# Two low columns ride behind the high columns: the z product's first token set at 260, 256 and 258 columns

## The chip, the cores and the metric

The kernel runs on one core of a Trainium2 chip. The metric is the device time of one launch in microseconds (us), as a median over runs. Inside a run, a profiler records every instruction of the core's engines: the tensor engine (PE, with its weight loads listed apart as PEld), the vector engine (DVE), the scalar engine (ACT), GpSimd (POOL) and the engine that issues most transfers (SP).

## The reference

One layer of a hybrid decoder: 16 meta tokens are put ahead of 1024 tokens, the 1040 rows are normalised, and one wide product `z` feeds two branches (windowed attention and a gated convolution), which are merged by gates. A convolutional feed-forward network follows.

```python
h = layer_norm(concatenate([meta, x], axis=1), in_ln_g, in_ln_b)
z = h @ w_in + b_in
q, k, v, c_in, gates = split(z)          # 512, 128, 128, 1024, 2048 columns
y_attn = swa_sink_attention(q, k, v, ...) @ w_attn_proj
c_val, c_gate = split(c_in)
y_conv = silu(layer_norm(causal_dwconv(c_val * sigmoid(c_gate)))) @ w_conv_proj
g_attn, g_conv = split(gates)
mixed = sigmoid(g_attn) * y_attn + sigmoid(g_conv) * y_conv
h = layer_norm(ALPHA * h + mixed @ w_out)
up = causal_dwconv(h @ ffn_w_up); u, g = split(up)
out = layer_norm(ALPHA * h + (gelu(g) * u) @ ffn_w_down)[:, 16:]
```

The meta rows are dropped from the output. Behind `z`, only the last two meta tokens (rows 14 and 15) are still needed for gates and queries, since the feed-forward convolution has 3 taps.

## The kernel before, in words

Products are computed in a reduced float32 type on PE, and each operand is split into a high part and a low part: high times high, high times low, low times high, three matmuls for each chunk of 128 contracted channels (function `product`, L303 to L316: L310 is high weights on high tokens, L314 high weights on low tokens, L315 low weights on high tokens). The contraction of 1024 channels has 8 chunks, so a set of tokens takes 24 matmuls, all summed in one PSUM tile.

The 30 tiles of 128 columns of `w_in` are the weights (`whi`, `wlo`), the normalised tokens, transposed, are the moving operand. They lie in two SBUF tiles, RHO for chunks 0 to 3 and RHC for chunks 4 to 7; `h0(k, hl, a, b)` (L267) gives the columns a to b of chunk k, high (hl 0) or low (hl 1). The columns of the first 272 tokens lie in a region of their own, one block of 272 words for each pair of chunk and part; the other 768 tokens lie in blocks of 768 words ahead of it. In the built program both tiles begin 64 bytes past a multiple of 128 bytes. So the second token set begins on such a multiple (word 16 + 768 i), and the first set's needed columns, from token 14, begin 72 or 8 bytes past one.

Tokens are taken in three sets, `ZG` = 0 to 272, 272 to 528, 528 to 1040. For queries 1 to 3 and the 16 gate tiles the first set begins at token 14 (`TG`), which makes it 258 columns; for the convolution's tiles it has 272. `z_group` (L318) takes a PSUM tile `ps_z`, of which there are 3 in turn, and hands it to an evacuation: a gate's is one ACT instruction with tanh and a store (L714, L715), a query's one ACT instruction (L362) and then a split into high (ACT, `qsh`) and low (DVE, `qsl`).

At the start of the program the order of work on PE, ACT and DVE is written out by hand (`in_order`). There, `parts(g, k)` (L510 to L517) splits the transposed tokens of a set into high and low parts, one cast and one subtraction for each chunk; the first set's parts (`FA` to RHO and RHC, 272 columns) are written into the row of the last set's (`tm`, 384 columns), while PE runs the first product of the last set (L550). After that a scheduler orders the work by ranks: the evacuations come first, the splits of weights (L279 on ACT, L282 on DVE) next, then attention, then the tiles of z, and the convolution's taps on DVE (L707, 120 instructions on 1026 columns) last. Attention's matmuls are set among the tiles of z.

Of the kernel before, what the change touches and what calls it, by code (L numbers as in the profile page):

```python
# [25 lines left out]
AF = mybir.ActivationFunctionType  # L26
OP = mybir.AluOpType
# [4 lines left out]
KC = D // P  # L32
NMETA = 16
S = 1024
T = S + NMETA
U0 = 14
U = T - U0
HD = 64
# [63 lines left out]
def tile_hybrid_layer(  # L102
# [3 lines left out]
    nc = tc.nc  # L106
# [5 lines left out]
    def load(o, i):  # L112
        return nc.sync.dma_start(out=o, in_=i)

    def store(o, i):

        return nc.scalar.dma_start(out=o, in_=i)

    def f32(ap):
        return ap.bitcast(F)  # L120

    def after(ins, first):

        tc.add_manual_dep(ins.ins, first.ins.name, mybir.DependencyInfo(
            mybir.DependencyClass.NoSync, mybir.DependencyReason.SCHED_ONLY), reason="order of work")

    @contextmanager
    def rank(p):

        saved = tc.cur_priority  # L130
        tc.cur_priority = p
        yield
        tc.cur_priority = saved
# [34 lines left out]
    start = ExitStack()  # L168
# [39 lines left out]
    def bcol(m):  # L208
        return colA[:, m:m + 1]
# [13 lines left out]
    qb = const.tile([P, 4], F, name="qb")  # L223
# [42 lines left out]

    def h0(k, hl, a, b):  # L267
        i = (k % 4) * 2 + hl
        o = 6196 + i * 272 if a < 272 else 16 + i * 768 - 272
        return (RHO if k < 4 else RHC)[:, o + a:o + b]  # L270


# [14 lines left out]
    def weights(shape, fill):  # L287
        fills[0] += 1
        n = fills[0]
        own = n == 3  # L290
        raw = sp.tile(shape, F, name="wr3") if own else wraw(shape)
        with rank({1: 13, 2: 18, 3: 17, 4: 23}.get(n, RK_SPLIT)):
            last_fill.append(fill(raw))
        hi, lo = (sp.tile(shape, R, name=t + "3") if own else wsp_p.tile(shape, R, name=t, tag=t)
                  for t in ("whi", "wlo"))
        if n <= 3:
            return hi, lo, raw
        with rank(RK_SPLIT):
            last_split.append(split(raw, hi, lo, True))
        return hi, lo  # L300
# [2 lines left out]

    def product(ps, terms, behind=None, lead=None):

        n = len(terms)
        if lead is not None:
            nc.tensor.matmul(ps[:, :64], terms[0][0], lead, start=True, stop=True)
        for i, (ah, al, bh, bl) in enumerate(terms):
            ins = nc.tensor.matmul(ps, ah, bh, start=i == 0, stop=False)  # L310
            chunks_done.append(ins)
            if i == 0 and behind is not None:
                after(ins, behind)
            nc.tensor.matmul(ps, ah, bl, start=False, stop=False)  # L314
            last = nc.tensor.matmul(ps, al, bh, start=False, stop=i == n - 1)  # L315
        return last  # L316

    def z_group(wt, g, a, b, evac):  # L318
        hi, lo = wt
        ps = pat.tile([P, 512], F, name="ps_z", tag="mm", bufs=3)  # L320
        product(ps[:, :b - a], [(hi[:, k], lo[:, k], h0(k, 0, a, b), h0(k, 1, a, b)) for k in range(KC)])
        with rank(RK_EVAC):
            evac(g, a, b, ps[:, :b - a])

    def z_tile(fill, groups, evac, wt=None):
        wt = wt or weights([P, KC, P], fill)
        for g, (a, b) in enumerate(groups):
            z_group(wt, g, a, b, evac)

    def in_cols(m):  # L330
        return lambda raw: load(raw, w_z[m])
# [5 lines left out]
    def stage(n):  # L337
        o = st_next[0] if st_next[0] + n <= 2040 else 0
        st_next[0] = o + n
        return FA[:, 4104 + o:4104 + o + n]  # L340
# [17 lines left out]

    def q_evac(r):
        def evac(g, a, b, ps):  # L360
            t = stage(b - a)
            nc.scalar.activation(t, ps, AF.Identity, bias=qb[:, r:r + 1], scale=HD ** -0.5)  # L362
            cut = b - a if g == 0 else 256
            for x in range(0, b - a, cut):
                parts_of(r, g, t[:, x:min(b - a, x + cut)], a + x)
        return evac

    def parts_of(r, g, t, a):
        n = t.shape[-1]
        h, l = (qsp.tile([P, 272], R, name=x, tag=x)[:, :n] for x in ("qsh", "qsl"))  # L370
        nc.scalar.copy(h, t)
        nc.vector.tensor_tensor(l, t, f32(h), OP.subtract)
        for hl, (put, x) in enumerate(((store, f32(h)), (load, f32(l)))):
            c = 0
            if g == 0:
                c = 2
                load(dram(qd, (hl * 4 + r) * 2, [[8 * U, P], [1, 2]]), x[:, :2])
            m = (n - c) // P
            i = (a - U0 + c) // P
            put(dram(qd, q_at(i) + (hl * 4 + r) * HD, [[8 * U, P], [4 * P, 2 * m], [1, HD]]),  # L380
                x[:, c:].rearrange("p (n q) -> p n q", q=HD))
# [13 lines left out]
    V = nc.vector  # L395
# [113 lines left out]
    def parts(g, *ks, hi_act=()):  # L509
        a, b = HG[g]  # L510
        for k in ks:
            tm = tms[g, k]
            if k in hi_act:
                ac(nc.scalar.copy(h0(k, 0, a, b), tm))
            else:
                dv(V.tensor_copy(h0(k, 0, a, b), tm))
            dv(V.tensor_tensor(h0(k, 1, a, b), tm, f32(h0(k, 0, a, b)), OP.subtract))  # L517

    first = [weights([P, KC, P], in_cols(m)) for m in (4, 5, 0)]
    evacs0 = [k_evac, v_evac, q_evac(0)]  # L520
# [11 lines left out]
    def span(i, g):  # L532
        a, b = HG[g]
        return (U0 if i == 2 and g == 0 else a), b
# [30 lines left out]
    def evac(g, *tiles):  # L565
        for i in tiles:
            a, b = span(i, g)
            with rank(RK_EVAC):
                evacs0[i](g, a, b, sums0[i])
# [50 lines left out]
    for k in range(8):  # L620
        scaled(1, k)
        parts(1, k, hi_act=(k,))
        if k == 1:
            whi0(1)
            wlo0(1)
        if k in (3, 6):
            stat(4, 6 if k == 3 else 7)
# [10 lines left out]
    for k in range(8):  # L638
        scaled(2, k)
        parts(2, k, hi_act=(1, 3, 5, 7))  # L640
        if k in (3, 4, 5, 6):
            parts(0, 2 * k - 6, 2 * k - 5)
# [5 lines left out]
    for a, b in ((0, 400), (400, J_LEN)):  # L648
        ps = pat.tile([P, 512], F, name="ps_v", tag="o" if a == 0 else "t", bufs=1 if a == 0 else 2)
# [20 lines left out]
    V = ap.tile([P, NB, NKV, 2, HD], R, name="v")  # L670
# [3 lines left out]
    bias = ap.tile([P, 2, NH // 2, KW], F, name="bias")  # L674
# [34 lines left out]
    def gate_tile(i):  # L709
        b2, m = divmod(i, KC)  # L710

        def gate_evac(g, a, b, ps):
            t = stage(b - a)
            nc.scalar.activation(t, ps, AF.Tanh, bias=bcol(14 + i), scale=0.5)  # L714
            store(sgd[b2, m, :, a - U0:b - U0], t)  # L715

        z_tile(in_cols(14 + i), TG, gate_evac)
# [28 lines left out]
    ps = pat.tile([P, 512], F, name="ps_vm", tag="t", bufs=2)  # L746
# [4 lines left out]
    for q4 in range(2):  # L751
        ps = pat.tile([P, 512], F, name="ps_v4", tag="t", bufs=2)
# [4 lines left out]
        for g in range(NKV):  # L757
            hi, lo = (V[:, q4 * 4:q4 * 4 + 4, g, i] for i in range(2))
# [35 lines left out]
    ps = pat.tile([P, 512], F, name="ps_s2", tag="t", bufs=2)  # L794
    for h in range(NH):
        g, r = divmod(h, 4)
        o = ps[:2, h * 16:(h + 1) * 16]
# [34 lines left out]
    for g in range(NKV):  # L832
        ps = pat.tile([P, 512], F, name="ps_t2", tag="t", bufs=2)
# [3 lines left out]
        hi, lo = (t[:16, g * 8:g * 8 + 8].rearrange("p (r q) -> p r q", r=4) for t in p2)  # L837
        nc.scalar.copy(hi, src)
        nc.vector.tensor_tensor(lo, src, f32(hi), OP.subtract)
    for g in range(NKV):  # L840
        o = po[:, g * 8:g * 8 + 8]
# [21 lines left out]
    for i in range(NB):  # L863
        for g in range(NKV):
# [299 lines left out]
    for m in range(KC):  # L1164
        hi, lo = weights([P, KC, P], lambda raw: load(raw, w_ab[m]))
# [403 lines left out]
    for c in range(FC):  # L1569
# [8 lines left out]
        for subs in passes:  # L1578
            last = subs == passes[-1]
            w_next = iter(range(7))  # L1580
            a, b = SUB[subs[0]][0], SUB[subs[-1]][1]
            i = max(a, 2)

            def at(t, a=a):
                return t[:, 254 + a:254 + b]
# [34 lines left out]
            ins = tt(c11[:, a:b], at(Z), u13[:, a:b], OP.add)  # L1620
# [23 lines left out]
            ins = tt(c22[:, i:b], c22[:, i:b], u13[:, i:b], OP.add)  # L1644
# [286 lines left out]
```

## Time and profile before

| | |
|---|---|
| median of 3 runs | 1236.19 us (1235.96 to 1236.53) |
| profiled execution, first to last instruction | 1234.6 us (its time around that is not listed; median less span is 1.6 us) |
| granted PE clock | 0.999 |
| PE busy | 1225.2 us, 99% |
| DVE busy | 1085.2 us, 88% |
| ACT busy | 584.7 us, 47% |
| PE in the stretch 55 to 405 us (tiles of z and attention) | 350.0 of 350.0 us |
| DVE in that stretch | 324.2 of 350.0 us |
| ACT in that stretch | 156.6 of 350.0 us |

[...] The distance from one start to the next is what a matmul costs in a dense row, and it is read from the list of instructions in order of time. In that list, equal instructions that follow each other share a row, and a figure in brackets is the idle time ahead of a row with what ended it. Some matmul records are missing from a trace.

### The profile page before, as it was taken

How to read it: one execution, taken by the hardware profiler on the slowest of the kernel's cores; microseconds unless marked ns; L12 is line 12 of the kernel's file. 1: busy time of each engine (PE TensorE's matmuls, PEld its weight loads, DVE VectorE, ACT ScalarE, POOL GpSimd, SP SyncE). 2: the span in 40 equal slices, each digit the busy share in tenths (PEclk: the TensorE clock that was granted, in tenths of full speed). 3: DMA queues.
4: the chain of work that ended last, by engine and by line, in shares of the span. 5: the costliest groups of instructions: out<-in, count | busy, mean ns of one | idle time of the engine just before them, and what ended most of it. 6: DMA issues, size and time to landing. Idle time of an engine off the chain costs nothing.

```text
span 1234.6 us, 21810 instructions
## 1 busy us (share of the span) xinstructions
PE 1225.2 (99%) x8568; PEld 1141.5 (92%) x8568; DVE 1085.2 (88%) x1842; ACT 584.7 (47%) x1065; POOL 15.6 (1%) x20
## 2 busy tenths in 40 slices
PE   9999999999999999999999999999999999999997
PEld 8999989999999999888999999999999998888886
DVE  8899989999879798659899999998999986996697
ACT  7532336654255223345755545555455554445331
POOL 1000000000000010000000000000000000000000
PEclk9999999999999999999999999999999999999999
DMA  7396834412255655322255555554455568988722
GB/s 282 74 298 151 210 98 116 127 55 73 82 158 163 183 140 144 104 85 87 66 171 207 191 187 205 188 183 142 172 203 190 178 239 304 391 315 312 256 86 85
DMA packets 109152, 213.02 MB, mean 173 GB/s; under 512 B 31883, under 2 KB 46779, under 8 KB 108922
## 3 DMA queue, kind: packets, MB, share of 16 engines
q1 hardware_dynamic: 93050, 200.56, 49.5%
q10 hardware_dynamic: 16000, 11.07, 2.9%
q8 instruction: 67, 1.10, 0.4%
q14 instruction: 35, 0.29, 0.1%
HBM read 149.98 MB, written 62.70 MB: 172 GB/s over the span
## 4 chain that ended last, share of the span: by engine, by line
PE 98%; DVE 1%; ACT 0%; issue 0%; DMA 0%; POOL 0%; DVEq 0%; POOLq 0%
PE px L1599 14%; PE py L1599 9%; PE ps_x L1745 9%; PE ps_z L315 8%; PE ps_z L314 8%; PE ps_z L310 8%; PE ps_z L1745 8%; PE pw L1599 5%; PE pz L1599 5%; PE ps_p L310 2%; PE ps_p L314 2%; PE ps_p L315 2%; PE ps_w L310 2%; PE ps_w L315 2%; PE ps_w L314 2%; PE ps_z L550 2%
## 5 line engine op out<-in xcount | busy, mean ns | idle before, releaser
L707 DVE SCALAR_TENSOR_TENSOR FA<-cin,cols,FA 128x1026 f32<-128x1026 f32 x120 | 152.2, 1277 | 0.9
L315 PE MATMUL ps_z<-RHO,wlo 128*128 128x256 f32 (+2 forms) x324 | 103.5, 320 | 0.0
L314 PE MATMUL ps_z<-RHO,whi 128*128 128x256 f32 (+2 forms) x324 | 103.4, 319 | 0.0
L315 PE MATMUL ps_z<-RHC,wlo 128*128 128x256 f32 (+2 forms) x324 | 103.4, 319 | 0.0
L314 PE MATMUL ps_z<-RHC,whi 128*128 128x256 f32 (+2 forms) x324 | 103.4, 319 | 0.0
L310 PE MATMUL ps_z<-RHO,whi 128*128 128x256 f32 (+2 forms) x324 | 103.3, 319 | 0.0
L310 PE MATMUL ps_z<-RHC,whi 128*128 128x256 f32 (+2 forms) x324 | 103.2, 319 | 0.0
L279 ACT CAST whi<-wr 128x1024 fp32r<-128x1024 f32 x37 | 38.9, 1050 | 107.4 <-PE ps_z L314 85.5
L1408 ACT CAST RHO<-wr 128x512 fp32r<-128x512 f32 x92 | 55.3, 619 | 25.3 <-DVE wr L1426 11.7
L1409 DVE TENSOR_TENSOR RHO<-wr,RHO 128x512 fp32r<-128x512 f32 x92 | 61.8, 684 | 5.1 <-ACT RHO L1408 5.0
L310 PEld LDWEIGHTS ps_z<-RHO,whi 128*128 128x128 f32 x324 | 60.9, 188 | 4.3
L314 PEld LDWEIGHTS ps_z<-RHO,whi 128*128 128x128 f32 x324 | 61.0, 188 | 4.2
L310 PEld LDWEIGHTS ps_z<-RHC,whi 128*128 128x128 f32 x324 | 60.9, 188 | 4.1
L314 PEld LDWEIGHTS ps_z<-RHC,whi 128*128 128x128 f32 x324 | 61.0, 188 | 4.0
L315 PEld LDWEIGHTS ps_z<-RHO,wlo 128*128 128x128 f32 x324 | 60.9, 188 | 4.0
L315 PEld LDWEIGHTS ps_z<-RHC,wlo 128*128 128x128 f32 x324 | 61.0, 188 | 3.9
L1426 DVE TENSOR_TENSOR wr<-wr 128x512 f32<-128x512 f32 x88 | 59.9, 681 | 0.2
L282 DVE TENSOR_TENSOR wlo<-wr,whi 128x1024 fp32r<-128x1024 f32 x35 | 42.7, 1220 | 11.8 <-ACT whi L279 11.4
L1611 ACT COPY FA<-px 128x514 f32<-128x514 f32 (+2 forms) x23 | 13.2, 572 | 70.7 <-PE px L1599 70.6
L1408 ACT CAST ws<-wr 128x512 fp32r<-128x512 f32 x60 | 36.1, 618 | 18.8 <-DVE wr L1426 10.7
L714 ACT ACTIVATE FA<-ps_z,cols 128x258 f32<-128x258 f32 (+2 forms) x48 | 26.1, 544 | 39.4 <-PE ps_z L315 36.6
L1599 PE MATMUL px<-OA,RHO 128*128 128x258 f32 (+1 forms) x336 | 43.8, 279 | 0.0
(491 smaller groups left out, 3488.2 us busy)
## 6 DMA issues: line engine op xcount, KB each, us to landing
wr<-in_w_up_dram SPq DMA_DIRECT2D x44, 512.0 KB, 4.6
wr<-in_w_z_dram SPq DMA_DIRECT2D x30, 512.0 KB, 3.9
fd<-FA SPq DMA_DIRECT2D x44, 256.0 KB, 2.4
OB<-in_w_down_dram SPq DMA_DIRECT2D x19, 512.0 KB
qt<-qd SPq DMA_DIRECT2D x28, 256.0 KB, 4.1
td<-OB SPq DMA_DIRECT2D x12, 512.0 KB
sums<-fd SPq DMA_DIRECT2D x12, 512.0 KB, 7.6
sd<-sums SPq DMA_DIRECT2D x12, 512.0 KB
```

The source lines that it names most:

```text
L279: ins = nc.scalar.copy(hi, raw)
L282: return (nc.vector if quick else nc.gpsimd).tensor_tensor(lo, raw, f32(hi), OP.subtract)
L310: ins = nc.tensor.matmul(ps, ah, bh, start=i == 0, stop=False)
L314: nc.tensor.matmul(ps, ah, bl, start=False, stop=False)
L315: last = nc.tensor.matmul(ps, al, bh, start=False, stop=i == n - 1)
L707: nc.vector.scalar_tensor_tensor(acc[c], cin[:, j:j + U], wc, acc[c], OP.mult, OP.add)
L714: nc.scalar.activation(t, ps, AF.Tanh, bias=bcol(14 + i), scale=0.5)
L1408: nc.scalar.copy(hi, src)
L1409: ins = nc.vector.tensor_tensor(lo, src, f32(hi), OP.subtract)
L1426: ins = nc.vector.tensor_tensor(*x)
L1599: ins = nc.tensor.matmul(o, x[:, ks], bmat(sub, q, hl, k), start=first and k + j == 0, stop=k == 3 and j == 2, skip_group_check=not first)
L1745: nc.tensor.matmul(bank[:, cs], l[:, ts], r[:, ws], start=first and a and x + k == 0, stop=z and x == len(ops) - 1 and k == 2, skip_group_ ...
```

## The change

For queries 1 to 3 and the 16 gate tiles, the first set is computed by matmuls of 260, 256 and 258 columns where there were three of 258. High weights run over the 258 high columns and, behind them, over the two low columns of tokens 14 and 15; the result of these two stands in PSUM columns 258 and 259. High weights then run over the 256 low columns of tokens 16 to 271, into PSUM columns 2 to 257. Low weights run over the 258 high columns as before. The columns streamed are 774 both ways.

So that the two low columns stand right behind the high ones, the first set's region has blocks of 274 and 272 words for high and low, 546 for a chunk. `parts(0, k)` copies the two columns, one more DVE instruction for each of the 8 chunks. The evacuation of such a set adds the two PSUM columns to the first two: ACT copies columns 258 and 259 to SBUF, DVE adds PSUM columns 0 and 1 to them, ACT puts these two through the function, and a second ACT instruction does the other 256. That makes, for each of the 19 tiles, two more ACT instructions and one DVE instruction that waits for ACT and is waited for by ACT.

```diff
     def h0(k, hl, a, b):
         i = (k % 4) * 2 + hl
-        o = 6196 + i * 272 if a < 272 else 16 + i * 768 - 272
+        o = 6196 + (k % 4) * 546 + hl * 274 if a < 272 or b <= 274 else 16 + i * 768 - 272
         return (RHO if k < 4 else RHC)[:, o + a:o + b]
...
     def product(ps, terms, behind=None, lead=None):
-        n = len(terms)
+        n, w = len(terms), ps.shape[-1]
+        cuts = ((0, w),) * 3 if terms[0][2].shape == terms[0][3].shape else ((0, w), (2, w - 2), (0, w - 2))
+        outs = [ps[:, x:y] for x, y in cuts]
...
-            ins = nc.tensor.matmul(ps, ah, bh, start=i == 0, stop=False)
+            ins = nc.tensor.matmul(outs[0], ah, bh, start=i == 0, stop=False)
...
-            nc.tensor.matmul(ps, ah, bl, start=False, stop=False)
-            last = nc.tensor.matmul(ps, al, bh, start=False, stop=i == n - 1)
+            nc.tensor.matmul(outs[1], ah, bl, start=False, stop=False)
+            last = nc.tensor.matmul(outs[2], al, bh[:, :outs[2].shape[-1]], start=False, stop=i == n - 1)
...
+        n = b - a
+        if a == U0:
+            n += 2
+            product(ps[:, :n], [(hi[:, k], lo[:, k], h0(k, 0, a, b + 2), h0(k, 1, NMETA, b)) for k in range(KC)])
...
+    def evacuate(t, ps, func, **kw):
+        n = t.shape[-1]
+        if n == 260:
+            t, e = t[:, :n - 2], t[:, n - 2:]
+            n -= 2
+            nc.scalar.copy(e, ps[:, n:n + 2])
+            nc.vector.tensor_tensor(e, e, ps[:, 0:2], OP.add)
+            nc.scalar.activation(t[:, 0:2], e, func, **kw)
+            nc.scalar.activation(t[:, 2:], ps[:, 2:n], func, **kw)
+        else:
+            nc.scalar.activation(t, ps, func, **kw)
+        return t
...
         def evac(g, a, b, ps):
-            t = stage(b - a)
-            nc.scalar.activation(t, ps, AF.Identity, bias=qb[:, r:r + 1], scale=HD ** -0.5)
+            t = evacuate(stage(ps.shape[-1]), ps, AF.Identity, bias=qb[:, r:r + 1], scale=HD ** -0.5)
...
             dv(V.tensor_tensor(h0(k, 1, a, b), tm, f32(h0(k, 0, a, b)), OP.subtract))
+            if g == 0:
+                dv(V.tensor_copy(h0(k, 0, b, b + 2), f32(h0(k, 1, U0, NMETA))))
...
         def gate_evac(g, a, b, ps):
-            t = stage(b - a)
-            nc.scalar.activation(t, ps, AF.Tanh, bias=bcol(14 + i), scale=0.5)
+            t = evacuate(stage(ps.shape[-1]), ps, AF.Tanh, bias=bcol(14 + i), scale=0.5)
             store(sgd[b2, m, :, a - U0:b - U0], t)
```

Three places show how the instructions stand. The first is DVE at the hand-written start, where the parts of the first set (`FA`) and of the last (`tm`) are made; L516 is the cast to high, L517 the subtraction that gives low. Before:

```order
L517 TENSOR_TENSOR RHO<-FA,RHO 128x272
L516 CAST RHO<-FA 128x272
L517 TENSOR_TENSOR RHO<-FA,RHO 128x272
L516 CAST RHC<-tm 128x384
L517 TENSOR_TENSOR RHC<-tm,RHC 128x384
L516 CAST RHO<-FA 128x272
L517 TENSOR_TENSOR RHO<-FA,RHO 128x272
```

The same place after the change, with L536 and L537 for the two instructions and L539 for the copy of two columns:

```order
L537 TENSOR_TENSOR RHO<-FA,RHO 128x272
L539 CAST RHO<-RHO 128x2
L536 CAST RHO<-FA 128x272
L537 TENSOR_TENSOR RHO<-FA,RHO 128x272
L539 CAST RHO<-RHO 128x2
L536 CAST RHC<-tm 128x384
L537 TENSOR_TENSOR RHC<-tm,RHC 128x384
L536 CAST RHO<-FA 128x272
L537 TENSOR_TENSOR RHO<-FA,RHO 128x272
L539 CAST RHO<-RHO 128x2
```

Nothing is moved there; a copy stands behind each of the 8 low parts, and all 8 stand ahead of the last subtraction of the last set (chunk 7).

The second place is PE at the first set of query 1. Before:

```order
L315 MATMUL ps_z<-RHC,wlo 128x512
L310 MATMUL ps_z<-RHO,whi 128x258
L314 MATMUL ps_z<-RHO,whi 128x258
L315 MATMUL ps_z<-RHO,wlo 128x258
L310 MATMUL ps_z<-RHO,whi 128x258
```

And after:

```order
L318 MATMUL ps_z<-RHC,wlo 128x512
L313 MATMUL ps_z<-RHO,whi 128x260
L317 MATMUL ps_z<-RHO,whi 128x256
L318 MATMUL ps_z<-RHO,wlo 128x258
L313 MATMUL ps_z<-RHO,whi 128x260
```

The number of matmuls is the same, 152 of each of the three kinds in all. Further on, among the tiles of z, the attention's matmuls stand up to a few microseconds of PE work later than before; behind the last tile of z the order on PE is the same as before.

The third place is ACT at the evacuations of query 2, set 0 and set 1. Before:

```order
L362 ACTIVATE FA<-ps_z,qb 128x258
L371 CAST qsh<-FA 128x258
L117 DMA qd<-qsh 128x4x64
L362 ACTIVATE FA<-ps_z,qb 128x256
L371 CAST qsh<-FA 128x256
```

After, where L338 is the copy of two columns, L340 their function, L341 the other 256 columns of set 0, and L343 set 1:

```order
L338 COPY FA<-ps_z 128x2
L343 ACTIVATE FA<-ps_z,qb 128x256
L340 ACTIVATE FA<-FA,qb 128x2
L341 ACTIVATE FA<-ps_z,qb 128x256
L391 CAST qsh<-FA 128x258
L391 CAST qsh<-FA 128x256
```

Set 0 leaves its PSUM tile behind set 1 here, and the split of set 0 stands behind both; L340 waits for DVE's addition (L339).

More of the change, by code (lines that the diff above doesn't have):

```diff
@@ L320, in z_group @@
         ps = pat.tile([P, 512], F, name="ps_z", tag="mm", bufs=3)
-        product(ps[:, :b - a], [(hi[:, k], lo[:, k], h0(k, 0, a, b), h0(k, 1, a, b)) for k in range(KC)])
-        with rank(RK_EVAC):
-            evac(g, a, b, ps[:, :b - a])
+        n = b - a
[3 more added lines that the diff above has]
+        else:
+            product(ps[:, :n], [(hi[:, k], lo[:, k], h0(k, 0, a, b), h0(k, 1, a, b)) for k in range(KC)])
+        with rank(RK_EVAC):
+            evac(g, a, b, ps[:, :n])
+    def evacuate(t, ps, func, **kw):
[7 more added lines that the diff above has]
+            nc.scalar.activation(t[:, 2:], ps[:, 2:n], func, **kw)
+        else:
+            nc.scalar.activation(t, ps, func, **kw)
+        return t
     def z_tile(fill, groups, evac, wt=None):
```

## The prediction

> **What bounds the kernel now.** I read the page's head and its chain first, then the busy time by stretches and the waits of PE, and last the list of instructions in order of time at the places that the change touches.
>
> ```profile
> span 1234.6 us, 21810 instructions
> PE 98%; DVE 1%; ACT 0%; issue 0%; DMA 0%; POOL 0%; DVEq 0%; POOLq 0%
> ```
>
> The chain that ended last is 98% PE. By stretches (columns: length, then busy time of PE, PEld, DVE, ACT and POOL with their instruction counts, PE clock, DMA share, GB/s):
>
> ```profile
> 0.00:55.00 55.00, 53.35 (x314) 49.57 (x314) 45.04 (x107) 38.09 (x69) 4.77 (x15) 1.00 0.53 182
> 55.00:405.00 350.00, 350.00 (x2376) 322.23 (x2375) 324.20 (x577) 156.63 (x362) 0.00 (x0) 1.00 0.51 140
> 405.00:1227.00 822.00, 821.52 (x5882) 769.57 (x5881) 712.10 (x1151) 388.74 (x632) 10.87 (x5) 1.00 0.54 186
> ```
>
> From 55 to 1227 us PE stands idle for half a microsecond. So the time is the sum of what PE's rows cost, start to start, plus the hand-written start. What makes a PE row cheaper is gained in full; what makes PE late by x anywhere ahead of 1227 us is lost in full, since no later idle time takes it up.
>
> **The z product: equal columns, one run of 256.** Around the change's matmuls, in order of time (start, recorded length):
>
> ```profile
> 101.05 0.29 PE L310 MATMUL ps_z<-RHO,whi 128*128 128x258 f32 x1
> ...
> 103.93 0.28 PE L310 MATMUL ps_z<-RHO,whi 128*128 128x256 f32 x1
> ...
> 106.65 0.39 PE L310 MATMUL ps_z<-RHO,whi 128*128 128x512 f32 x1
> ...
> 112.14 0.29 PE L310 MATMUL ps_z<-RHO,whi 128*128 128x258 f32 x1
> ```
>
> Each stretch holds 24 matmuls. 258 columns cost (103.93 - 101.05)/24 = 120.0 ns, 256 cost (106.65 - 103.93)/24 = 113.3 ns, 512 cost (112.14 - 106.65)/24 = 228.8 ns. Two columns are dearer by 6.7 ns, where the slope from 256 to 512 is 115.5/256 = 0.45 ns a column. So there is a step of about 5.8 ns, and the question is what sets it off: the count 258, or the place where the columns begin. A second place with 256 columns, near the end, decides that better:
>
> ```profile
> 1219.30 0.88 PE L1745 MATMUL ps_x<-OC,RHC 128*128 128x256 f32 x6
> ...
> 1226.86 0.52 PE L1745 MATMUL ps_z<-RHO 128*128 128x256 f32 x3
> ```
>
> Between these two starts stand 63 matmuls of 256 columns (6, 6, 6, 12, 3 twice, less the last 3): (1226.86 - 1219.30)/63 = 120.0 ns. The count is 256 and the step is there. In the built program the moving columns of those begin 64 bytes past a multiple of 128, those of the second token set on a multiple. The new 256-column run begins at token 16 of the low block, 24, 32, 40 or 48 bytes past a multiple, chunk by chunk. It is nearest to the L1745 rows, so I take 120.0 ns and no gain. The other end is 113.3 ns: 19 tiles x 8 chunks = 152 matmuls x 6.7 ns = 1.0 us gained. The 260-column run costs two columns more, 152 x 2 x 0.45 ns = 0.14 us; the low end is 0, if the step holds a few columns for nothing. The blocks' new places shift every start of the first set, in the convolution's 272-column runs too (8 tiles x 24). Nothing here prices that; the nearest rows are the two costs of 256 columns, and since none of these runs begins on a multiple of 128 bytes before or after, I take 0.
>
> [...]
>
> **The start: eight copies on DVE, in the open.** Between 41 and 49 us DVE makes the parts of the last set and the first in one row, with PE behind it:
>
> ```profile
> 41.35 0.44 DVE L517 TENSOR_TENSOR RHO<-FA,RHO 128x272 fp32r<-128x272 f32 x1
> 41.71 0.30 DVE L516 CAST RHO<-FA 128x272 fp32r<-128x272 f32 x1
> 42.04 0.44 DVE L517 TENSOR_TENSOR RHO<-FA,RHO 128x272 fp32r<-128x272 f32 x1
> 42.40 0.35 DVE L516 CAST RHC<-tm 128x384 fp32r<-128x384 f32 x1
> ...
> 48.73 0.55 DVE L517 TENSOR_TENSOR RHC<-tm,RHC 128x384 fp32r<-128x384 f32 x1
> 49.20 1.29 DVE L479 TENSOR_SCALAR gb<-gb 128x1024 f32<-128x1024 f32 x2
> ```
>
> No row in that stretch has idle time ahead of it. PE at the same place (L550, the last set's first product):
>
> ```profile
> 48.48 0.51 PE L550 MATMUL ps_z<-RHO,whi 128*128 128x384 f32 x2
> 48.83 0.34 PE L550 MATMUL ps_z<-RHO,wlo 128*128 128x384 f32 x1
> 49.01 0.77 PE L550 MATMUL ps_z<-RHC,whi 128*128 128x384 f32 x2
> 49.62 0.34 PE L550 MATMUL ps_z<-RHC,wlo 128*128 128x384 f32 x1
> ```
>
> A pair usually takes 0.35 us to the third matmul (48.48 to 48.83); the pair of chunk 7 takes 0.61. Its second matmul reads the low part that DVE finishes at 49.28. So PE already waits 0.26 us for DVE here, and whatever DVE is given ahead of that subtraction delays PE by as much. All eight copies stand ahead of it.
>
> A copy reads what the subtraction ahead of it writes, so it must wait for its end. An independent successor starts 0.36 us after a subtraction (41.35 to 41.71), though that lasts 0.44; a dependent one starts 0.03 us after the end of its predecessor (41.71 + 0.30 to 42.04). The copy thus starts at 0.47 and costs 0.11 us before it begins. Then its own length:
>
> ```profile
> 31.31 0.16 DVE L436 SCALAR_TENSOR_TENSOR t<-mv,r 128x3 f32<-128x3 f32 x1
> 31.51 0.16 DVE L437 SCALAR_TENSOR_TENSOR t<-t,r 128x3 f32<-128x3 f32 x1
> ...
> 256.95 0.15 DVE L895 SCALAR_TENSOR_TENSOR sm<-sm,nsink 128x4 f32<-128x4 f32 x1
> 257.02 1.22 DVE L282 TENSOR_TENSOR wlo<-wr,whi 128x1024 fp32r<-128x1024 f32 x1
> ```
>
> With a dependent successor a tiny DVE instruction costs 0.20 us to the next start, with an independent one 0.07. The next cast or subtraction does not read the copy, so I take 0.09, a little above the lower row since the copy is of another kind. Together 0.20 us, times 8 = 1.6 us on PE. The bounds are 8 x 0.18 = 1.4 and 8 x 0.31 = 2.5 us; below them lies 0, if the profile's reading of who waits for whom is wrong here.
>
> [...]
>
> **The evacuations.** Each of the 19 tiles adds an ACT copy, a DVE addition and an ACT instruction on two columns, where ACT is busy 156.6 of 350 us. Their cover is the ring of three PSUM tiles: set 0's tile is wanted again only when PE has run sets 1 and 2, 2.72 + 5.49 = 8.2 us later. What could eat that is lateness of DVE, with ACT standing behind it in its row (set 1's evacuation, the weights' split and exponentials). In the waits of the stretch 60 to 405 us (total, times, longest):
>
> ```profile
> ACT s L902 <- DVE sm L895: 11.6, 6, 4.5
> ```
>
> The longest time that ACT stood for DVE is 4.5 us, and PE did not feel it. Behind ACT stands the weights' split; its slack:
>
> ```profile
> 359.40 1.05 ACT L279 CAST whi<-wr 128x1024 fp32r<-128x1024 f32 x1 [4.37 <-PE ps_z L314]
> ...
> 360.48 1.23 DVE L282 TENSOR_TENSOR wlo<-wr,whi 128x1024 fp32r<-128x1024 f32 x1 [0.68 <-ACT whi L279]
> ...
> 371.23 0.29 PE L310 MATMUL ps_z<-RHO,whi 128*128 128x258 f32 x1
> ```
>
> The low weights are done at 361.7 and first wanted with this tile's third matmul behind 371.23, 9.5 us later. I cost the evacuations at nothing under this cover; without it every microsecond beyond 8 is PE's. The first set's query stores move behind set 1's evacuation, 24 x 113.3 ns = 2.7 us later, ahead of the loads of `qt`; the attention's first matmuls stand 23 rows of PE later as well. SP and POOL get no more to do.
>
> The nearest place where a late DVE would show is the hand-over to the projections:
>
> ```profile
> 405.91 1.23 DVE L282 TENSOR_TENSOR wlo<-wr,whi 128x1024 fp32r<-128x1024 f32 x1 [1.17 <-ACT whi L279]
> ...
> 410.58 0.55 DVE L1057 TENSOR_TENSOR OA<-OB,OA 128x384 fp32r<-128x384 f32 x1
> ...
> 412.78 0.28 PE L310 MATMUL ps_p<-OA,whi 128*128 128x256 f32 x1
> ```
>
> DVE stood 1.17 us for ACT (which waited for PE), and the last split of the attention's output ends 1.65 us ahead of the PE row that stands out of its place for it. A lateness of 2.8 us passes.
>
> **Sum.** 0 for the 256 columns, +0.14 for the 260, +1.6 for the start: the span goes from 1234.6 to 1236.3 us. The median stands 1.6 us above the profiled span, which I carry over: 1236.19 + 1.7 = 1237.9 us. A difference under 0.2% (2.5 us) can hardly be told from no change, and this is 0.14%.
>
> **Rivals.**
>
> *The count sets the step, so 256 columns gain wherever they begin.* For it: every 256-column row of z is cheap. Against it: the 63 matmuls of L1745. Time: 1237.9 - 1.0 = 1236.9 us.
>
> *The copies are hidden.* PE then loses nothing at the start, if DVE has some slack that the list does not show. Against it: no idle time ahead of a DVE row from 41.35 to 49.2, and PE's pair at 49.01. Time: 1236.3 us without and 1235.3 us with the gain of 256 columns.
>
> *The addition stands behind taps, and PSUM tiles come back late* (slower). The place is the tiles of z where DVE has the convolution's taps. In the changed order an addition can stand behind 6 taps and a weight split:
>
> ```profile
> L707 DVE SCALAR_TENSOR_TENSOR FA<-cin,cols,FA 128x1026 f32<-128x1026 f32 x120 | 152.2, 1277 | 0.9
> ```
>
> That is 6 x 1.2 + 1.2 = 8.4 us (1.28 long, 1.2 from start to start), just above the cover of 8.2. It decides from the point where DVE falls a whole tile behind PE. With six such tiles and 0.5 to 1 us each: 3 to 6 us, 1241 to 1244 us. Against it: ACT's longest wait for DVE was half of that.
>
> **How the numbers follow.** Forecast 0.57; the count rival 0.20; hidden copies 0.10; late PSUM tiles 0.10; 0.03 for something that makes it clearly faster. The forecast's own bounds run from 1237.6 to 1238.8; the range takes in the count rival and most of the hidden copies: 1235.9 to 1239.2 us. Faster by over 0.2% (under 1233.7) has 0.02; slower by over 0.2% (above 1238.7) takes the late tiles and the upper end of the copies, 0.14; the rest, 0.84, is within 0.2%.
>
> **What would show it.** Right: in the new profile the 260, 256 and 258 columns stand about 360 ns apart from one triple to the next; the copies of L539 add some 0.2 us each; chunk 7's pair of the last set comes about 1.6 us later and the first tile of z starts near 56.8 us; PE has no idle time from there to the end. Wrong: a triple of 353 ns (the count rival); a first tile of z near 55.2 (hidden copies); PE idle ahead of a first set's matmul with a wait for DVE or ACT (late tiles).

## The result and the profile after

The changed kernel takes 1239.73 us (median of 7 runs, 1239.54 to 1240.09) against 1236.15 us of the kernel before in the same comparison: 1.0029 times, 95% interval 1.0018 to 1.0040. It is slower by 3.6 us, where I forecast 1.7 and a range that ended at 1239.2.

The head of the page and, by stretches, the z stage and what follows it, in the profile after (columns as in the prediction; the stretches begin with the first tile of z and the first projection):

```profile
span 1238.0 us, 21895 instructions
```

```profile
56.50:408.20 351.70, 351.70 (x2373) 323.88 (x2373) 323.98 (x595) 160.50 (x398) 0.00 (x0) 1.00 0.50 139
408.20:1230.00 821.80, 821.38 (x5879) 769.35 (x5878) 713.01 (x1153) 389.04 (x632) 10.82 (x5) 1.00 0.54 187
```

PE still has no idle time in the z stage (351.70 of 351.70 us busy), at a granted clock of 1.00. Two places in the list of instructions tell where the time went. The kernel before, PE in order of time:

```profile
55.18 0.37 PE L310 MATMUL ps_z<-RHO,whi 128*128 128x272 f32 x1
...
162.66 0.28 PE L310 MATMUL ps_z<-RHO,whi 128*128 128x256 f32 x1
...
165.49 0.39 PE L310 MATMUL ps_z<-RHO,whi 128*128 128x512 f32 x1
...
404.87 0.28 PE L310 MATMUL ps_p<-OA,whi 128*128 128x258 f32 x1
```

The changed kernel, the same view:

```profile
56.57 0.37 PE L313 MATMUL ps_z<-RHO,whi 128*128 128x272 f32 x1
...
103.02 0.28 PE L313 MATMUL ps_z<-RHO,whi 128*128 128x260 f32 x1
...
105.87 0.28 PE L313 MATMUL ps_z<-RHO,whi 128*128 128x256 f32 x1
...
108.70 0.40 PE L313 MATMUL ps_z<-RHO,whi 128*128 128x512 f32 x1
...
114.20 0.29 PE L313 MATMUL ps_z<-RHO,whi 128*128 128x260 f32 x1
...
408.24 0.28 PE L313 MATMUL ps_p<-OA,whi 128*128 128x258 f32 x1
```

- The first tile of z starts 56.57 - 55.18 = 1.39 us later. Since the last set's first product (L572, before L550) stood 0.16 us earlier than before, at 25.35 against 25.51 us, the stretch between the two has grown by 1.55 us.
- The z stage, from there to the first projection, has grown from 404.87 - 55.18 = 349.69 to 408.24 - 56.57 = 351.67 us, by 1.98 us, without a wait.
- Behind it nothing changes: the last matmul comes 3.33 us later than before, the first projection 3.37.

Inside the z stage the first set behaves: (105.87 - 103.02)/24 = 118.8 ns. The surprise is the second set, 256 columns from places that the change does not touch: (108.70 - 105.87)/24 = 117.9 ns, where the prediction's rows gave 113.3. And this dear pace stands in the trace of before as well: (165.49 - 162.66)/24 = 117.9 ns, the same line, tile shape and starts. I had read the pace from one tile.

So I took the mean start-to-start distance inside each run of 24 from both traces (a distance over 1.2 times the run's median is left out, since there other matmuls or missing records stand). In the table, "cheap" counts the second sets with a mean under 114.6 ns, and "sum" is what the four means would change: difference to before x 24 x number of runs.

| | first set, 258 (19 runs) | first set, 272 (8) | second set, 256 (27) | cheap | third set, 512 (27) | sum |
|---|---|---|---|---|---|---|
| before | 119.9 ns | 125.7 | 115.2 | 15 | 229.6 | |
| changed | 119.5 | 126.9 | 118.0 | 0 | 229.9 | +2.0 us |

The second set makes 2.75 ns x 24 x 27 = 1.8 us of the 2.0. It has two paces, 113.3 and 117.8 ns, and before it was in the cheap one in 15 tiles and in the dear one, or between, in 12; changed, it is in the dear one in all. Each trace is of one execution, and so is each count of cheap tiles.

### The profile page after: what moved, and what is told of

Its sections match the earlier page's. It is cut to its first block, busy times and chain, and to the rows that moved or that the text cites. A ratio compares the mean times of both kernels' runs of the same rounds, so it can differ in the third digit from the quotient of the medians.

```text
span 1238.0 us, 21895 instructions
## 1 busy us (share of the span) xinstructions
PE 1227.2 (99%) x8568; PEld 1142.5 (92%) x8568; DVE 1087.4 (88%) x1869; ACT 588.9 (48%) x1102; POOL 15.6 (1%) x20
## 4 chain that ended last, share of the span: by engine, by line
PE 94%; DVE 1%; ACT 0%; issue 0%; DVEq 0%
PE px L1620 14%; PE py L1620 9%; PE ps_x L1766 9%; PE ps_z L313 8%; PE ps_z L317 8%; PE ps_z L318 8%; PE ps_z L1766 8%; PE pw L1620 5%; PE pz L1620 5%; PE ps_p L313 2%; PE ps_p L318 2%; PE ps_p L317 2%; PE ps_w L317 2%; PE ps_w L313 2%; PE ps_w L318 2%; PE ps_o L949 1%
## 5 line engine op out<-in xcount | busy, mean ns | idle before, releaser
L313 PE MATMUL ps_z<-RHO,whi 128*128 128x256 f32 (+2 forms) x324 | 104.1, 321 | 0.0
L317 PE MATMUL ps_z<-RHO,whi 128*128 128x256 f32 (+1 forms) x324 | 103.8, 320 | 0.0
L317 PE MATMUL ps_z<-RHC,whi 128*128 128x256 f32 (+1 forms) x324 | 103.7, 320 | 0.0
L313 PE MATMUL ps_z<-RHC,whi 128*128 128x256 f32 (+2 forms) x324 | 103.4, 319 | 0.0
L1430 DVE TENSOR_TENSOR ws<-wr,ws 128x512 fp32r<-128x512 f32 x60 | 40.4, 684 | 3.5 <-ACT ws L1429 3.5
```

Source lines behind the costliest of these rows:

```text
L313: ins = nc.tensor.matmul(outs[0], ah, bh, start=i == 0, stop=False)
L317: nc.tensor.matmul(outs[1], ah, bl, start=False, stop=False)
L1430: ins = nc.vector.tensor_tensor(lo, src, f32(hi), OP.subtract)
```

## Experiments: which part of the change costs it

Three theories, named in the expectations: the new places of the blocks (P), the unequal lengths with what belongs to them (C), or what the start leaves behind (H). The count of 16 cheap tiles in the expectations is a rougher reading of the 15 above.

**Places alone.**

```diff
-        o = 6196 + i * 272 if a < 272 else 16 + i * 768 - 272
+        o = 6196 + (k % 4) * 546 + hl * 274 if a < 272 else 16 + i * 768 - 272
```

> The kernel before with the blocks at the changed kernel's places (546 words from chunk to chunk, low block 274 behind the high one) and nothing else: all runs of the first set keep 258 columns, no copies, no split evacuation. In the trace of the changed kernel the second token set (256 columns, places unchanged) is issued every 117.7 ns in all 27 tiles; before it was 113.3 ns in 16 tiles and 117.7 ns in 11, which makes most of 2.0 us. Theory P (the first set's new start places set the dearer pace): 1238.2 us, second set 117.7 ns throughout. Theory C (the unequal lengths 260, 256, 258 or the shifted PSUM columns set it): 1236.2 us, second set as before. Theory H (what the start leaves behind sets it): 1236.2 us, as before.

Measured: 1238.57 us, 2.37 above the kernel before (in brackets here and below, the ratio to it with its 95% interval: 1.0019, 1.0010 to 1.0028). PE in order of time:

```profile
104.36 0.28 PE L310 MATMUL ps_z<-RHO,whi 128*128 128x256 f32 x1
...
107.19 0.40 PE L310 MATMUL ps_z<-RHO,whi 128*128 128x512 f32 x1
```

(107.19 - 104.36)/24 = 117.9 ns; no second set is cheap. The places alone bring the loss in the z stage; C and H are not needed for it. With three runs of 258 the first set stands at 120.2 ns, so the cut itself gains a little, 0.7 ns x 24 x 19 = 0.3 us.

**Copies out of the way.** In the changed kernel:

```diff
-            if g == 0:
-                dv(V.tensor_copy(h0(k, 0, b, b + 2), f32(h0(k, 1, U0, NMETA))))
...
+    for k in range(8):
+        dv(V.tensor_copy(h0(k, 0, 272, 274), f32(h0(k, 1, U0, NMETA))))
     lagged(2, (0, 2, 1), range(12))
```

> The changed kernel with its eight copies of two columns moved on DVE behind the last part of the start, so that they stand between no two parts that PE waits for. My term for the copies is 1.6 us, the traces side by side show 1.5 us between 25 and 56 us: 1238.1 to 1238.2 us with the second token set still at 117.7 ns (theories P and C). Theory H: the entry into the z stage is then as before, the second set falls back to 113.3 ns at least up to 140 us, and the time is 1236.2 to 1237.3 us. If the copies were not what delayed the start, 1239.7 us.

Measured: 1238.04 us, 1.69 below the changed kernel and 1.84 above the kernel before (1.0016, 1.0007 to 1.0025). The first tile of z starts at 55.00 us, and the second set is at 118.0 ns, none cheap. So the copies' place was worth 1.6 to 1.7 us, and it has nothing to do with the pace (H falls). On DVE in this run all eight stand in one row and cost 0.07 us each:

```profile
49.02 0.37 DVE L664 CAST RHO<-RHO 128x2 fp32r<-128x2 f32 x4
49.29 0.37 DVE L664 CAST RHC<-RHC 128x2 fp32r<-128x2 f32 x4
49.57 1.29 DVE L499 TENSOR_SCALAR gb<-gb 128x1024 f32<-128x1024 f32 x2
```

**The cut at the old places.** In the changed kernel:

```diff
-        o = 6196 + (k % 4) * 546 + hl * 274 if a < 272 or b <= 274 else 16 + i * 768 - 272
+        o = 6196 + i * 272 if a < 272 or b <= 274 else 16 + i * 768 - 272
```

> The changed kernel with cut, copies and split evacuation, but with the blocks at the places of before (544 words from chunk to chunk); the two extra columns stand where the low parts of tokens 0 and 1 were, which are so left out of the convolution's columns. Theory P: the dear pace goes, 1237.7 us. Theory C: 1239.7 us, second set 117.7 ns throughout. Theory H: 1239.7 us.

Measured: 1238.67 us, 2.47 above the kernel before (1.0021, 1.0012 to 1.0029), halfway between the theories; with 1.55 us for the copies, 0.9 remain. PE in order of time, two tiles that follow each other:

```profile
105.34 0.28 PE L313 MATMUL ps_z<-RHO,whi 128*128 128x256 f32 x1
...
108.17 0.40 PE L313 MATMUL ps_z<-RHO,whi 128*128 128x512 f32 x1
...
116.56 0.28 PE L313 MATMUL ps_z<-RHO,whi 128*128 128x256 f32 x1
...
119.29 0.39 PE L313 MATMUL ps_z<-RHO,whi 128*128 128x512 f32 x1
```

117.9 ns in the one, (119.29 - 116.56)/24 = 113.8 in the next. In the convolution's tiles, whose first set is not cut, the cheap pace is back (113.3 ns in the first four); in the tiles with a cut first set both paces occur, at first in turn. This alone does not show that equal work takes either pace, since the weights of successive tiles lie in two buffers in turn. The trace of before shows it inside one set, with one pair of weight tiles and one PSUM tile, where eight of attention's matmuls stand in the row:

```profile
173.99 0.28 PE L310 MATMUL ps_z<-RHO,whi 128*128 128x256 f32 x1
...
174.78 0.28 PE L314 MATMUL ps_z<-RHO,whi 128*128 128x256 f32 x1
174.90 1.03 PE L835 MATMUL ps_t<-cols,s 128*16 128x128 f32 x8
...
175.89 0.28 PE L310 MATMUL ps_z<-RHO,whi 128*128 128x256 f32 x1
...
177.18 0.28 PE L315 MATMUL ps_z<-RHC,wlo 128*128 128x256 f32 x1
```

Ahead of them a matmul takes (174.78 - 173.99)/7 = 112.9 ns, behind them (177.18 - 175.89)/11 = 117.3 ns. All five second sets of that trace that enter at the cheap pace and are broken by attention's matmuls change over in this way. So the pace depends on what ran just before, and P and C are both too simple.

## Experiments: which starts

**On a multiple of 128 bytes.** My prediction put the step between 113.3 and 120 ns down to starts off such a multiple. The kernel before with one number changed, in two runs, of which the second gives the trace:

```diff
-        o = 6196 + i * 272 if a < 272 else 16 + i * 768 - 272
+        o = 6178 + i * 272 if a < 272 else 16 + i * 768 - 272
```

> The kernel before with its first-set blocks moved 18 words down, so that the high block's 258-column runs begin on a multiple of 128 bytes and the low block's 64 bytes past one. My prediction took the step of 5.8 ns for a matter of the start: then two of three 258-column runs fall from 120.0 to about 114.2 ns, 19 tiles x 16 x 5.8 ns = 1.8 us less, 1234.4 us, if the second set keeps its pace, and 1236.2 us if it falls into 117.7 ns throughout. If the step is a matter of the count 258, 1236.2 us, or 1238.2 us with the second set at 117.7 ns.

> The kernel before with the 258-column runs of the high block on a multiple of 128 bytes once more, for its trace: 1238.4 us. If the second set's pace is what it loses, 117.7 ns in (nearly) all 27 tiles and the first set near 120 ns; if the first set itself became dearer, above 122 ns there and the second set as before.

Measured: 1238.38 us (1.0017, 1.0008 to 1.0026) and 1238.32 us (1.0018, 1.0008 to 1.0028). The second run's PE:

```profile
101.90 0.28 PE L310 MATMUL ps_z<-RHO,whi 128*128 128x258 f32 x1
...
104.75 0.28 PE L310 MATMUL ps_z<-RHO,whi 128*128 128x256 f32 x1
...
107.58 0.40 PE L310 MATMUL ps_z<-RHO,whi 128*128 128x512 f32 x1
```

258 columns take (104.75 - 101.90)/24 = 118.8 ns although two of three now begin on a multiple; 119.3 over all tiles. A start on a multiple is thus not enough to bring them to 113.3. The second set is in the dear pace in all 27, though it begins on a multiple as before.

That does not clear the start of all blame. In the trace of before, the feed-forward's 256-column matmuls (L1599) begin on multiples in the built program, and 72 of them in one row are cheap:

```profile
622.46 1.52 PE L1599 MATMUL py<-RX,RHO 128*128 128x256 f32 x12
...
630.62 1.59 PE L1599 MATMUL px<-RHC,RHO 128*128 128x258 f32 x12
```

They take (630.62 - 622.46)/72 = 113.3 ns, where the prediction's 63 of L1745, 64 bytes past one, take 120.0. No run here moved either of these two.

**Swapped by 64 bytes, and drifting.** The same line with 6180 in place of 6196; and with `6196 + (k % 4) * 546 + hl * 272`.

> The kernel before with its first-set blocks 16 words (64 bytes) lower: the high block's 258-column runs begin 8 bytes past a multiple of 128 and the low block's 72 past one, which is 72 and 8 before. If only the start within 64 bytes counts, 1236.2 us and the second set at 113.3 ns in most tiles. If the start within 128 bytes counts, the dear pace, 117.7 ns in all tiles, and about 1238.2 us as in the runs with moved blocks.

> The kernel before with 546 words from chunk to chunk but the low block still 272 behind the high one, so that all three runs of a chunk begin at one place within 64 bytes, 8 bytes later in each chunk. If the drift from chunk to chunk sets the dear pace: 1238.2 to 1238.6 us. If it is the shift between the high and the low block: 1236.2 us, the second set at 113.3 ns in most tiles.

Measured: 1237.54 us (1.0011, 1.0003 to 1.0020), no second set cheap, but the first set at 119.4 ns; and 1238.37 us (1.0015, 1.0006 to 1.0024), one cheap. The dear pace needs neither a drift nor a shift: of the placements tried with uncut runs, only that of before holds the cheap pace in more than one tile.

**The low run on a multiple of 128 bytes.** In the kernel with the cut at the old places, 6192 for 6196.

> The cut kernel with blocks 544 words apart (the extra two columns again in place of the low parts of tokens 0 and 1, which are left out of the convolution's columns), placed so that the 256-column run with low tokens begins on a multiple of 128 bytes. This is the other end of my term for the cut: if such a run costs 113.3 ns where it now takes 118.5 to 120 ns, 152 x 5 to 6.7 ns = 0.8 to 1.0 us less than the same kernel with that run 16 bytes past a multiple (1238.67 us): 1237.7 to 1237.9 us. If the pace hangs on the run of starts and not on this one, no gain from it: 1238.5 to 1239.6 us, the latter with 117.7 ns in all second sets.

Measured: 1239.73 us (1.0030, 1.0018 to 1.0041), the second of the two outcomes. The 256-column run between its neighbours of 260 and 258 costs 120.1 ns on a multiple, against 118.5 in the changed kernel off one (means over the sets that nothing interrupts). The gain of 1.0 us that was the other end of my term is not there.

## Experiments: a pace that is handed on

Theory O: a run's own starts set its pace. Theory R: it takes it over from how the run ahead leaves PE.

**A short matmul between the first and the second set**, in the kernel before and in the changed one with late copies:

```diff
-        product(ps[:, :b - a], [(hi[:, k], lo[:, k], h0(k, 0, a, b), h0(k, 1, a, b)) for k in range(KC)])
+        product(ps[:, :b - a], [(hi[:, k], lo[:, k], h0(k, 0, a, b), h0(k, 1, a, b)) for k in range(KC)],
+                lead=h0(0, 0, 272, 336) if a == 272 else None)
```

> The kernel before with one more matmul of 64 columns ahead of each second set (27 in all; its sums are overwritten by the product's first matmul). By itself it takes about 27 x 0.03 to 0.06 us = 0.8 to 1.6 us. Theory O: 1237.0 to 1237.8 us and the second set as before. Theory R: the pace of the second set changes in some tiles, 1236 to 1240 us, whichever way the short one leaves PE.

> The changed kernel with the copies behind the start (1238.04 us) and the same 64-column matmul ahead of each second set. Theory O: 1238.8 to 1239.6 us, 117.7 ns throughout. Theory R: at least some second sets at 113.3 ns; all of them would give 1238.0 + 0.8 to 1.6 - 2.9 us, 1235.9 to 1236.7 us.

Measured: 1241.25 us (1.0041, 1.0028 to 1.0054) and 1240.92 us (1.0039, 1.0025 to 1.0053). The kernel before with it:

```profile
104.69 0.19 PE L308 MATMUL ps_z<-RHO,whi 128*128 128x64 f32 x1
104.72 0.36 PE L310 MATMUL ps_z<-RHO,whi 128*128 128x256 f32 x1
104.92 0.28 PE L314 MATMUL ps_z<-RHO,whi 128*128 128x256 f32 x1
...
107.64 0.40 PE L310 MATMUL ps_z<-RHO,whi 128*128 128x512 f32 x1
```

The changed kernel with it:

```profile
104.89 0.20 PE L311 MATMUL ps_z<-RHO,whi 128*128 128x64 f32 x1
104.92 0.36 PE L313 MATMUL ps_z<-RHO,whi 128*128 128x256 f32 x1
105.12 0.28 PE L317 MATMUL ps_z<-RHO,whi 128*128 128x256 f32 x1
...
107.72 0.39 PE L313 MATMUL ps_z<-RHO,whi 128*128 128x512 f32 x1
```

From the second matmul of the set on: (107.64 - 104.92)/23 = 118.3 ns and (107.72 - 105.12)/23 = 113.0 ns. The roles are turned over. Before goes from 15 cheap tiles to none, the changed kernel from none to 18 of 27, with the set's own starts, columns and weights as they were. Theory O falls. The times are no better because the short one is dear: it takes 0.03 us, but the matmul behind it has its successor 0.20 us later instead of 0.118, so 0.03 + 0.20 - 0.118 = 0.11 us in all and 27 x 0.11 = 3.0 us. I had priced it at 0.8 to 1.6 us, by its own time alone. The trace of before has one such place, which cost as much: L308 with 64 columns at 407.76 us, the matmul behind it at 407.80, that one's successor at 408.00. With the 1.9 us from the second set's pace this gives 4.9 of the 5.0 us that the first of the two lost. The second one's times spread over 1.9 us (1239.70 to 1241.55); the 18 tiles are those of its profiled execution, at 1239.70.

**Last two matmuls of the first set exchanged**, at no extra work; in the changed kernel with late copies, and as a control in the kernel before (shown):

```diff
+            if i == KC - 1 and ps.shape[-1] in (258, 272):
+                nc.tensor.matmul(ps, al, bh, start=False, stop=False)
+                last = nc.tensor.matmul(ps, ah, bl, start=False, stop=True)
+                continue
```

> The changed kernel with the copies behind the start (1238.04 us, second set at 117.7 ns in all 27 tiles), and in each first set the last two of its 24 matmuls exchanged (low weights first, then the run with low tokens); same matmuls, starts and sums. If the pace is handed on by how the first set ends: the second set changes over in some tiles, down to 1238.0 - 27 x 0.106 - 0.2 = 1235.0 us if in all. If the change itself (lengths, PSUM columns, evacuation) sets it: 1238.0 us.

> The control: the kernel before with the last two matmuls of each first set exchanged. If the pace is handed on by how the first set ends: the 16 second sets at 113.3 ns may fall to 117.7 ns, up to 1238.0 us, or the other 11 rise to the cheap one, down to 1235.0 us. If not: 1236.2 us.

Measured: 1237.88 us (1.0014, 1.0006 to 1.0023) with 3 cheap tiles, and 1237.62 us (1.0011, 1.0002 to 1.0020) with 5. The control moves by 1.4 us from an exchange of two matmuls of equal size, which speaks for R. The changed kernel stays dear in most tiles.

**Sets in another order, and other bases.** The second and third sets exchanged (`ZG` ending in 528 to 1040, then 272 to 528), in the kernel before and in the changed one with late copies; and the latter with its blocks at 6188 and 6180 in place of 6196.

> The kernel before with the second and third token sets exchanged in every tile: first set, then the 512-column set, then the 256-column one; the same matmuls, starts and columns. Theory O (a run's own starts set its pace): the 256-column runs keep their share of 113.3 and 117.7 ns, 1236.2 us. Theory R (a run takes over its pace from where the run ahead of it left PE, and what was ahead so far was the first set): the shares change; all 27 at 113.3 ns give 11 x 0.105 us less, 1235.0 us, all at 117.7 ns give 16 x 0.115 us more, 1238.0 us.

> The changed kernel with the copies behind the start (1238.04 us as it was) and the second and third sets exchanged as in the run before this. Theory O: 1238.0 us, all 256-column runs at 117.7 ns. Theory R: the run ahead is now the 512-column set with its starts of before; the dear pace need not stay, down to 1238.0 - 27 x 0.106 = 1235.2 us if all 27 fall to 113.3 ns.

> The changed kernel with the copies behind the start, its first-set blocks 8 words (32 bytes) lower. If the pace is handed on by where the first set's runs begin: it may change over, 1235.0 us with all second sets at 113.3 ns, 1238.0 us with none; the five other placements tried so far gave the dear pace, so I hold 1238.0 us for three times likelier. If the change itself sets it: 1238.0 us.

> As the run before this with the blocks 16 words (64 bytes) lower than in the changed kernel: 1235.0 us with all second sets at 113.3 ns, 1238.0 us with none, the latter three times likelier.

Measured: 1236.80 us (1.0005, 0.9996 to 1.0013) with 11 cheap; 1238.67 us (1.0020, 1.0011 to 1.0028) with 2 cheap; 1238.35 us (1.0018, 1.0009 to 1.0026) with none; 1238.30 us (1.0017, 1.0008 to 1.0025) with 1. Order and base move single tiles between the paces. The first of the four is 0.6 us above the kernel before, within an interval that includes no difference; the other three stay dear. They say little more than that.

Over all these runs but the two with the short matmul, which are worked out above, the sum of the result's table holds. Difference to before as measured, and as the four means give it (plus 1.55 us where the copies stand at their place in the start):

| run | measured | from the means |
|---|---|---|
| changed kernel | +3.6 us | +2.0 + 1.55 |
| places alone | +2.4 | +2.3 |
| copies late | +1.8 | +2.0 |
| cut at old places | +2.5 | +1.1 + 1.55 |
| starts on 128, again | +2.2 | +2.1 |
| swapped by 64 bytes | +1.4 | +1.6 |
| drift alone | +2.2 | +2.4 |
| low run on 128 | +3.6 | +2.2 + 1.55 |
| sets exchanged, before | +0.6 | +0.5 |
| sets exchanged, changed | +2.5 | +2.2 |
| last two exchanged, changed / before | +1.7 / +1.4 | +1.6 / +1.5 |
| base 6188 / 6180 | +2.2 / +2.1 | +2.0 / +1.9 |

## Experiments: why 256 columns have two paces

Each matmul of z has a load of 128 x 128 weights (1944 of each in the z stage of before). The dear short matmul led me to a guess that no run shows: that this load takes about as long as 256 columns do. In the kernel before and, likewise, in the changed one with late copies:

```diff
         for i, (ah, al, bh, bl) in enumerate(terms):
+            if short and i:
+                ps, bh, bl = ps[:, :short], bh[:, :short], bl[:, :short]
```

> The kernel before with the second set's matmuls of chunks 1 to 7 on 224 columns in place of 256; the last 32 columns of the set are so left out of those chunks. [...] If the load of the weights sets it: 113 ns or a little more, with or without the dear runs, 1235.0 to 1236.2 us.

> The same in the changed kernel with the copies behind the start (1238.04 us, 117.7 ns); the last 32 columns of the second set are left out of chunks 1 to 7. [...] If the load of the weights alone sets it, the two kernels now have the same spacing, near 113 ns in all 27 tiles: 1235.0 us. [...]

Measured: 1234.90 us (0.9992, 0.9983 to 1.0001) and 1234.35 us (0.9985, 0.9976 to 0.9993). The kernel before with 224 columns:

```profile
104.12 0.27 PE L312 MATMUL ps_z<-RHO,whi 128*128 128x224 f32 x1
...
106.46 0.40 PE L312 MATMUL ps_z<-RHO,whi 128*128 128x512 f32 x1
```

The changed one with 224 columns:

```profile
104.17 0.27 PE L316 MATMUL ps_z<-RHO,whi 128*128 128x224 f32 x1
...
106.50 0.40 PE L316 MATMUL ps_z<-RHO,whi 128*128 128x512 f32 x1
```

(106.46 - 104.12)/21 = 111.4 and (106.50 - 104.17)/21 = 111.0 ns; in both kernels every run whose 21 matmuls stand in one row has a mean of 111.2 to 111.4. An eighth fewer columns save 2 ns of 113.3, and the two paces are gone. By the prediction's 0.45 ns a column, the slope from 256 to 512, the 32 columns would have saved an estimated 14 ns. So from 256 to 224 columns the spacing hardly follows the columns. That the load of the weights sets it instead is not shown, since no run changed the weights' size; the trace of before records 188 ns for one load of the z product, while the next one starts 0.11 us after it (103.93 and 104.04 us). What is shown: with 224 columns one pace, with 256 two, and which of the two a set takes changes with what runs ahead of it (15 cheap tiles to none and none to 18 with the short matmul). Why there are two is not shown, and the guess does not explain the rows of L1745, which have 256 columns and one pace of 120.0 ns.

## Why the prediction was wrong, point by point

- **PE is the bound and a loss is never made up**: right. The z stage grew by 1.98 us and the start by 1.39, and the last matmul came 3.33 us later.
- **The start, eight copies, +1.6 us**: right, term by term. 1.55 us in the traces, 1.69 when the copies were moved. On DVE in the profile after:

```profile
41.19 0.43 DVE L537 TENSOR_TENSOR RHO<-FA,RHO 128x272 fp32r<-128x272 f32 x1
41.66 0.17 DVE L539 CAST RHO<-RHO 128x2 fp32r<-128x2 f32 x1
41.74 0.30 DVE L536 CAST RHO<-FA 128x272 fp32r<-128x272 f32 x1
```

  The copy starts 0.47 us after the subtraction as worked out, and the next cast 0.08 us later (I took 0.09): 0.11 + 0.08 = 0.19 us each. PE now shows the waits that I read out of its pair before:

```profile
PE ps_z L572 <- DVE RHC L537: 0.4, 1, 0.4
...
PE ps_z L572 <- DVE RHC L536: 0.4, 1, 0.4
```

- **The evacuations, 0**: right. ACT waits for the additions, PE waits for nothing:

```profile
L340 ACT ACTIVATE FA<-FA,cols 128x2 f32<-128x2 f32 x16 | 4.7, 295 | 9.5 <-DVE FA L339 7.2 <-DVE pl L940 1.2 <-DVE FA L729 0.4
```

- **The cut, 0 for the 256 columns and +0.14 for the 260**: right in size (the first set went from 119.9 to 119.5 ns, 0.2 us gained), but partly by luck: at the old places the same cut costs 0.9 us (0.3 in the first set, 0.65 in the second). The reason is not borne out either: I put the step down to starts off a multiple of 128 bytes, from rows near the end of the kernel, but on such a multiple 258 columns still took 119.3 ns, and 256 among longer neighbours 120.1.
- **The step that failed** is the sentence "Nothing here prices that; ... I take 0" on the blocks' new places. Alone they cost +2.4 us. In the changed kernel the z stage lost 2.0, and putting the old places back took only 1.1 us off, since there the cut turns part of the second sets over by itself. The loss is not in the runs whose starts move but in the run behind them, whose starts stay: a place that I never looked at, since no line of the change touches it. The trace of before did price it: the second set has two paces there, 4.5 ns apart, and 15 tiles that could fall from the one to the other are worth 15 x 24 x 4.5 ns = 1.6 us. I read one tile and took it for all: the prediction's sentence that "every 256-column row of z is cheap" fails for 12 of the 27 sets. Why the new places leave PE so that the next set is dear stays open.
- **The rivals**: the count does not give the gain (256 columns among 260 and 258 cost 118.5 ns), the copies are not hidden, and no PSUM tile came back late. The true case was not among them. It lies on the slow side, for which I had the wrong mechanism. The signs of being right that the prediction named came true (triples of 3 x 119.5 = 358.6 ns, copies of 0.19 us, the first tile of z at 56.57 us, PE never idle in the z stage): none of these signs looks at the second set.

## What to carry to other kernels

Before a dense row of matmuls is priced, compare the same run in every tile of the trace, not in one: where equal work from equal places shows two paces, as 113.3 and 117.8 ns here, a neighbour's change can move it from one to the other (15 cheap tiles to none here), and the distance between them times the number of runs is a bound that belongs into the range. A tuned kernel may hold the cheap pace by the accident of how its runs follow each other, so an edit of places alone wants a measurement of the runs behind it. What a tiny instruction costs has to be read where it stands: the same copy cost 0.19 us in the start, behind the subtraction that it waits for, and 0.07 in a row of its own kind, and 64 columns of matmul, with 0.03 us to the next start, cost 0.11 us.

## What the runs showed of the hardware that I had not expected

- In the second sets that nothing interrupts, the 24 matmuls of 256 columns, each with a load of 128 x 128 weights, stood 113.3 to 113.5 ns apart in the mean in 14 sets of the trace of before, and 117.8 in 3; in the trace after they stood 117.8 to 118.0 ns apart in all 16. With 224 columns the means were 111.2 to 111.4 ns, and the uncut runs of 258 had means of 119.3 to 120.2 ns over the 19 tiles.
- One matmul of 64 columns put ahead of such a set made the row 0.11 us longer, three quarters of it on the matmul behind (0.20 us to its successor in place of 0.118), and left none of 15 cheap tiles cheap in the kernel before and 18 of 27 cheap, of none, in the changed one.
